# A hybrid decoder layer on eight cores: x0 first on the DMA engines, w_up casts moved out of the way of tile 3's residuals, and new engines for the last additions

## The chip, the cores and the metric

One Trainium2 chip, all 8 cores, one launch. Each core computes the same program on its own share of the tokens, with no traffic between cores. The metric is the device time in microseconds (us) of the slowest core. Some executions fall into a slow state, in which the cores of one die (cores 0 to 3 or 4 to 7) show a lower granted clock and run some per cent longer. Fast runs are compared with fast runs.

## The reference, cut to what matters

One layer: a token mixer (pooling and short convolution, merged by sigmoid gates), then a gated ConvFFN, each between two RMS norms.

```python
h = rmsnorm(x, g_pre_mix)
z = h @ w_in                                   # 1024 -> 4096 columns: 32 blocks of 128
... pooling mixer a, short convolution b ...
merged = sigmoid(ga) * a + sigmoid(gb) * b
x = x + rmsnorm(merged @ w_o, g_post_mix)      # needs x again: the residual
h = rmsnorm(x, g_pre_ffn)
upc = causal_dwconv(h @ w_up)                  # 44 blocks of 128 columns, in 22 pairs gate/value
y = (silu(gate) * val) @ w_down
x = x + rmsnorm(y, g_post_ffn)
```

All inputs are fp32. Weights become bf16 on their way into the core's memory, by casting DMAs that GpSimd issues.

## The kernel before

A core has 2080 tokens, in five tiles for the mixer (tile 0 of 512 tokens, tiles 1 to 4 of 392) and six for the FFN (344 each, without the first 16 tokens). A small scheduler orders the operations per engine; `after=[...]` holds one back until another is done. `L` is 4, the last mixer tile. Cuts are marked.

```python
def wload(buf, src, m, after=()):      # one casting DMA of a weight block, issued by GpSimd (L482)
    ...
def wup(n):                            # the next n of the 44 w_up blocks
    ...
    for k in range(i, hi):
        pool_dma(W_UP.ap(k), w_up[k], [], [W_UP.t(k)], 128 * BL * 4, mx=2048, after=[last_pe[0]])

# the start: x0 in five pieces through SP, w_in through GpSimd, 60 warm-up matmuls
PARTS0 = ((0, 2), (2, 2), (4, 2), (6, 1), (7, 1))
...                                    # xs0[q]: the load of piece q
wload(W_IN, w_in, 0)
warm(60)
for i in range(1, 16):
    wload(W_IN, w_in, i, after=[last_pe[0] if i < 3 else xs0[1]])
... w_pool, w_in 16 to 31, w_co, then tile 1's x in four plain loads, all after xs0[1] ...

def B(t):                              # merge: gates, sigmoids, products
    for m in range(8):
        ...
        merge(t, m, *g[m])
        if t == L:
            wup(1)

for i in range(16):                    # the input projection of the last tile
    F_block(L, i)
    wup(1)
    if i == 4:
        WO(L - 1)                      # tile 3's output projection
        epi(L - 1)                     # its norm and residual: loads x of tile 3 again through GpSimd
small_states()
B(L)
WO(L, split=True, hook=lambda: wup(1))
...
for t in range(NTB):                   # the FFN
    for j in range(FC):                # 22 pairs
        pair(t, j)                     # reads w_up blocks 2j and 2j+1
        if t == 0:
            wup(1)
        if 20 <= 22 * t + j < 28:
            epi_x(L, 22 * t + j - 20)
        if (t, j) in ((0, 9), (0, 11), (0, 14), (0, 16), (0, 19), (0, 21), (1, 1), (1, 3)):
            wdn()                      # one of 8 w_dn blocks, 704 KB each
        ...
# the last additions: chunks 0,1 by an accumulating DMA, 2,3 by GpSimd, 4 to 7 by VectorE in PSUM
steps = ((0, 2, None, "acc"), (2, 2, None, "pool"), (4, 2, 0, "dve"), (6, 2, 2, "dve"))
```

All matmuls have line L469, since one helper records them.

## Time and profile before

Median 821.01 us (820.97 to 821.67). The spans in the traces below are shorter than the times of the same runs (820.1 against 821.65 here). I cut each core's span at five landmarks and averaged each stretch over the eight cores:

| stretch | before, us |
|---|---|
| start to first gate after tile 0 (L700) | 68.7 |
| to the end of tile 3's output projection (L732) | 214.8 |
| to the first pair of the FFN (L817) | 56.2 (core 0: 57.7) |
| to the last normalisation, after the last matmul (L520) | 467.6 |
| to the end of the span | 11.2 |

This is the view by tile, core 7 of the kernel before, from 340 to 400 us. It gives the number of issues with their shortest, median and longest duration in ns, the first and the last issue, and the time to landing.

```profile
L482 POOL DMA_DIRECT2D big<-w_up x12: 713/747/750, 341.5 to 369.1; - x12
DMA to landing us min/median/max: 7.3/10.8/14.2
```

The last block goes out at 369.1 us and lands at 378.9. The pair that reads it, pair 21, begins at about 388 us on this core (I count the 16 matmuls of each pair from the first at 338.35 us): 9 us to spare, and 8 to 10 us over the cores. No core spends any time waiting for w_up.

### The profile page before, as it was taken

The numbers are of one execution on the slowest core, as the hardware profiler recorded it, in microseconds if no ns is written. First come the engines' busy times: TensorE is split into PE (matmuls) and PEld (weight loads), VectorE is DVE, ScalarE is ACT, GpSimd is POOL, SyncE is SP. The second block draws the span as 40 slices with busy tenths as digits, with TensorE's granted clock in tenths as the row PEclk, the third lists the DMA queues.
The fourth block names the chain that finished last, engine by engine and source line by source line (L and its number), as shares of the span: only waits on it lengthen the run. The fifth ranks groups of instructions, "written<-read, shape, count | busy, mean of one in ns | idle before, by whom it ended". The sixth has DMA issues, their size and how long they took to land.

```text
span 820.1 us, 16719 instructions; the slowest of 8 cores (817.4 to 820.1 us)
## 1 busy us (share of the span) xinstructions
PE 798.2 (97%) x5118; PEld 498.9 (61%) x5118; DVE 563.4 (69%) x1054; ACT 450.7 (55%) x903; POOL 259.9 (32%) x296
## 2 busy tenths in 40 slices
PE   7999999999999998999999999999999999999994
PEld 5454455555555554666666666666666666666662
DVE  3896547877977595588986486568566765785722
ACT  3533375676475544686754475456556555765532
POOL 6542002002101261499532252225222522242221
PEclk9999999999999999999999999999999999999998
DMA  9999706567117799999960132015101500040063
GB/s 182 201 160 156 152 20 136 148 164 157 41 36 158 109 171 208 169 159 171 183 113 1 35 46 53 1 36 70 36 2 36 70 2 1 6 66 2 1 133 77
DMA packets 63735, 75.18 MB, mean 92 GB/s; under 512 B 3072, under 2 KB 59264, under 8 KB 63632
## 3 DMA queue, kind: packets, MB, share of 16 engines
q0 software_dynamic: 41440, 44.97, 38.9%
q1 hardware_dynamic: 22208, 29.14, 12.8%
q8 instruction: 44, 0.72, 0.3%
q14 instruction: 43, 0.35, 0.2%
HBM read 81.53 MB, written 22.90 MB: 127 GB/s over the span
## 4 chain that ended last, share of the span: by engine, by line
PE 90%; DMA 4%; DVE 2%; issue 2%; POOL 1%; ACT 1%; DVEq 0%; ACTq 0%; POOLq 0%
PE ps L469 90%; DMA big<-xT 4%; POOL big L482 1%; DVE big L549 0%; DVE big L783 0%; DVE big L821 0%; ACT big L520 0%; DVE big L509 0%; DVEq L1078 0%; DVE big L578 0%; ACT L520 0%; DVE big L658 0%; DVE big L867 0%; ACT big L848 0%; ACT big L768 0%
## 5 line engine op out<-in xcount | busy, mean ns | idle before, releaser
L469 PE MATMUL ps<-big 128*128 128x346 bf16 (+5 forms) x5118 | 798.2, 319 | 10.6 <-POOL big L922 2.9
L469 PEld LDWEIGHTS ps<-big 128*128 128x128 bf16 x5118 | 498.9, 98 | 309.6 <-issue 15.8
L821 DVE SCALAR_TENSOR_TENSOR big<-ps,big 128x344 f32<-128x344 f32 (+1 forms) x528 | 281.1, 569 | 94.8 <-ACT big L817 74.9
L835 POOL TENSOR_TENSOR big<-big 128x344 bf16<-128x344 f32 x132 | 125.5, 952 | 258.5 <-DVE big L821 186.2
L817 ACT ACTIVATE big<-ps,big 128x344 f32<-128x344 f32 (+1 forms) x264 | 139.4, 541 | 67.5 <-PE ps L469 61.7
L834 ACT ACTIVATE big<-big 128x344 f32<-128x344 f32 x132 | 64.6, 489 | 47.9 <-DVE big L821 45.9
L700 ACT ACTIVATE big<-ps 128x392 f32<-128x392 f32 (+1 forms) x80 | 38.9, 512 | 51.8 <-PE ps L469 34.7
L480 POOL DMA_DIRECT2D big<-xT x16 | 15.8, 997 | 153.4 <-DVE big L713 147.0
L845 ACT ACTIVATE big<-ps,big 128x344 f32<-128x344 f32 x48 | 26.0, 546 | 58.8 <-PE ps L469 55.8
L482 POOL DMA_DIRECT2D big<-w_up x44 | 33.3, 758 | 64.6 <-PE ps L469 52.8
L713 DVE SCALAR_TENSOR_TENSOR big<-ps,big 128x392 f32<-128x392 f32 (+1 forms) x40 | 25.8, 645 | 33.7 <-PE ps L469 31.4
L509 DVE TENSOR_TENSOR big<-big 128x1568 bf16<-128x1568 bf16 (+3 forms) x28 | 24.5, 875 | 32.2 <-ACT big L732 26.0
L851 DVE TENSOR_TENSOR big<-big 128x688 bf16<-128x688 bf16 x17 | 8.8, 518 | 41.5 <-ACT big L848 41.5
L480 POOL DMA_DIRECT2D yT<-big x21 | 27.3, 1523 | 31.0 <-DVE big L867 17.3
L730 ACT ACTIVATE big<-ps,big 128x392 f32<-128x392 f32 (+1 forms) x40 | 24.5, 613 | 13.0 <-PE ps L469 12.9
L606 DVE TENSOR_TENSOR big<-big 128x406 f32<-128x406 f32 (+7 forms) x50 | 29.8, 598 | 1.5 <-ACT big L628 0.2
L482 POOL DMA_DIRECT2D big<-w_in x32 | 23.2, 743 | 20.6 <-DMA big<-w_in 10.9
L575 ACT ACTIVATE big<-big 128x392 f32<-128x392 f32 (+1 forms) x20 | 12.7, 638 | 30.6 <-DVE big L664 30.5
L768 ACT ACTIVATE big<-big 128x784 bf16<-128x784 f32 (+1 forms) x20 | 17.8, 891 | 18.5 <-DMA big<-xT 16.0
L578 DVE SCALAR_TENSOR_TENSOR big<-big 128x392 f32<-128x392 f32 (+1 forms) x40 | 25.5, 644 | 3.6 <-ACT big L575 3.0
L848 ACT ACTIVATE big<-ps 128x344 bf16<-128x344 f32 x48 | 21.6, 451 | 10.4 <-PE ps L469 10.2
L719 DVE TENSOR_TENSOR big<-big 128x392 bf16<-128x392 f32 (+1 forms) x40 | 24.9, 631 | 2.3
(62 smaller groups left out, 353.4 us busy)
## 6 DMA issues: line engine op xcount, KB each, us to landing
big<-w_up POOLq DMA_DIRECT2D x44, 256.0 KB, 10.0
big<-w_in POOLq DMA_DIRECT2D x32, 256.0 KB, 22.6
yT<-big POOLq DMA_DIRECT2D x21, 344.0 KB, 6.2
big<-xT POOLq DMA_DIRECT2D x16, 392.0 KB, 8.9
yT<-big SPq DMA_DIRECT2D x8, 784.0 KB, 8.5
big<-w_dn POOLq DMA_DIRECT2D x8, 704.0 KB, 14.1
big<-xT SPq DMA_DIRECT2D x6, 784.0 KB, 6.2
big<-h2T SPq DMA_DIRECT2D x6, 692.0 KB, 5.8
```

The costliest lines, as they stand in the source:

```text
L469: ins = e.matmul(o, lhsT=l, rhs=x, start=(start and i == 0), stop=(stop and i == last))
L480: return S.add("pool", lambda e: e.dma_start(out=out, in_=in_, accum_op=ALU.add, max_dma_last_dim=mx), r, w, dma=True, byts=byts, pri=pri, ...
L482: return S.add("pool", lambda e: e.dma_start(out=out, in_=in_, max_dma_last_dim=mx), r, w, dma=True, byts=byts, pri=pri, after=after)
L578: dve(lambda e, k=k: e.scalar_tensor_tensor(out=cv, in0=p[:, 2 + k + lo:2 + k + N], scalar=cc(C_WC + 4 * k + c), in1=cv, op0=ALU.mult, op1 ...
L606: dve(lambda e, nx=nx, cur=cur, s=s, a2=a2: e.tensor_tensor(out=nx[:, a2:W], in0=cur[:, a2:W], in1=cur[:, a2 - s:W - s], op=ALU.add), [ct] ...
L700: act(lambda e, b=b, g=g: e.activation(out=GT[t].ap[:, g, lo:N], in_=bank(b, N, lo), func=AF.Sigmoid), [("ps", b)], [GT[t].t(g, 1)], N, ps ...
L713: dve(lambda e: e.scalar_tensor_tensor(out=A_, in0=bank(bp, N, lo), scalar=cc(C_PS + m), in1=A_, op0=ALU.mult, op1=ALU.mult), [("ps", bp), ...
L817: act(lambda e, b=b, fj=fj, tt=tt: e.activation(out=tt[:, 0:n], in_=bank(b, n), func=AF.Copy, scale=cc(C_WF + fj)), [("ps", b), KCST], [to ...
L821: dve(lambda e, b=b, fj=fj, tt=tt, k=k: e.scalar_tensor_tensor(out=tt[:, 0:n], in0=ps[:, b * 512 + k:b * 512 + k + n], scalar=cc(C_WF + 44 ...
L834: act(lambda e: e.activation(out=g, in_=g, func=AF.Silu), [T.t(0, 1)], [T.t(0, 1)], NB, tab="silu")
L835: S.add("pool", lambda e: e.tensor_tensor(out=gb.ap[:, j, :], in0=g, in1=v, op=ALU.mult), [T.t()], [gb.t(j, 1)], dur=NB * 2.17 + 100)
L845: act(lambda e: e.activation(out=Y.ap[:, m, :], in_=bank(b, NB), func=AF.Copy, scale=cc(C_G4 + m)), [("ps", b), KCST], [Y.t(m, 1)], NB, ps ...
```

## The change

The intent: let x0's first half have the DMA engines to itself; keep w_up casts out of GpSimd's queue while tile 3's residuals are loaded through the same queue; spread the work of `epi_x` among the first pairs of FFN tile 1; and end without an accumulating DMA.

```diff
-            steps = ((0, 2, None, "acc"), (2, 2, None, "pool"), (4, 2, 0, "dve"), (6, 2, 2, "dve"))
+            steps = ((0, 2, None, "pool"), (2, 1, None, "pool"), (4, 2, 0, "dve"), (6, 2, 2, "dve"), (3, 1, 4, "dve"))
... (the "acc" branch removed)
-    wload(W_IN, w_in, 0)
     warm(60)
-    for i in range(1, 16):
-        wload(W_IN, w_in, i, after=[last_pe[0] if i < 3 else xs0[1]])
+    for i in range(16):
+        wload(W_IN, w_in, i, after=[xs0[1 if i else 0]])
@@ merge loop
-            if t == L:
-                wup(1)
+            if t == L and m > 0:
+                wup(2)
@@ last tile
     for i in range(16):
         F_block(L, i)
-        wup(1)
+        if i < 7:
+            wup(1)
@@ pairs
+    EPX = (20, 21, 22, 23, 25, 26, 28, 29)
-            if 20 <= 22 * t + j < 28:
-                epi_x(L, 22 * t + j - 20)
+            if 22 * t + j in EPX:
+                epi_x(L, EPX.index(22 * t + j))
... (the last load of X1 takes all 8 chunks instead of 6)
```

More of the change, by code (lines that the diff above doesn't have):

```diff
@@ L872, in epi_y @@
                 yk, xk = Y.ap[:, k:k + n, :], X1.ap[:, k:k + n, :]
-                if how == "acc":
-                    pool_dma(yT[:, k:k + n, lo:lo + NB], yk, [Y.t(k, n)] + [("y", a, 0) for a in tiles_a(lo, lo + NB)],
-                             [("yo", t, k)], 2 * 128 * n * NB * 4, acc=True)
-                    continue
                 if how == "pool":
@@ L1065, in build_nc @@
     lo = T0B + (NTB - 1) * NB
-    sp_dma(X1.ap[:, 2:8, :], yT[:, 2:8, lo:lo + NB], [("y", a, q) for a in tiles_a(lo, lo + NB) for q in range(2)],
-           [X1.t(2, 6)], 128 * 6 * NB * 4)
+    sp_dma(X1.ap, yT[:, :, lo:lo + NB], [("y", a, q) for a in tiles_a(lo, lo + NB) for q in range(2)],
+           [X1.t()], 128 * KC * NB * 4)
     for m in range(8):
```

## The prediction

> **What bounds the kernel now.** I read the list of cores first, since the slowest core sets the time:
>
> ```profile
> core 0: 820.1 us, clock 0.994
> core 3: 819.0 us, clock 0.996
> core 7: 819.0 us, clock 0.995
> ```
>
> The eight spans run from 817.4 to 820.1 us; the timed 821.0 is the slowest span plus 0.9. The page gives TensorE 798.2 busy of 820.1 us, so everything else is worth at most the other 21.9 us. The table of waits says where TensorE stands still (line, releaser, us in total, times, longest), and the chain in order of time (start, length, what) says how two of those waits came about:
>
> ```profile
> PE ps L469 <- POOL big L922: 2.9, 1, 2.9
> PE ps L469 <- DVE big L509: 2.3, 1, 2.3
> PE ps L469 <- ACT big L940: 1.8, 2, 1.1
> PE ps L469 <- DVE big L964: 1.1, 1, 1.1
> ...
> PE ps L469 <- DVE big L821: 0.9, 1, 0.9
> ```
>
> The chain:
>
> ```profile
> 14.39 12.74 DMA big<-xT
> ...
> 29.53 7.14 PE ps L469 x42
> ...
> 298.36 19.45 DMA big<-xT
> ...
> 318.84 0.99 DVE big L509
> ...
> 320.63 80.94 PE ps L469 x525
> ```
>
> L940 squares the pieces of tile 0, L964 scales tile 1: both wait for transfers. The L509 wait of 2.3 us ends at 320.63: the last residual transfer of tile 3 took 19.45 us. The same residuals of tile 2, with nothing beside them, took 7.7 us (median of the DMA view, 180 to 192 us). The slices of 2 us after that wait (window, its length, PE busy, weight loads, DVE, ACT, POOL, then the granted clock, DMA share, GB/s) show a second cost:
>
> ```profile
> 318.00:320.00 2.00, 0.34 (x3) 0.00 (x0) 1.05 (x2) 1.51 (x3) 0.34 (x1) 1.00 0.91 110
> 320.00:322.00 2.00, 1.36 (x8) 0.84 (x9) 1.90 (x4) 0.00 (x0) 0.00 (x0) 0.95 1.00 156
> 322.00:324.00 2.00, 2.00 (x7) 0.91 (x6) 0.71 (x2) 1.66 (x2) 0.00 (x0) 0.50 1.05 186
> 324.00:326.00 2.00, 2.00 (x10) 1.04 (x9) 1.08 (x3) 1.88 (x4) 0.72 (x1) 0.70 1.09 224
> 326.00:328.00 2.00, 2.00 (x14) 1.18 (x13) 2.00 (x5) 1.81 (x4) 0.00 (x0) 1.00 1.11 296
> ```
>
> The clock is 0.50 and 0.70 in two slices: [...]from the clocks, 0.1+1.0+0.6 = 1.7 us. I take 1.5. The other seven cores wait 0.8 to 1.8 us at this place and keep clock 1.00. Core 0 is the slowest because of this place.
>
> [...]the 512 KB quarters of x0 go through SP at 205 and 192 GB/s (4 to 6 and 6 to 8 us) while a w_in cast issued by GpSimd at 1.6 us is in flight, against 339 GB/s at 26 to 28 us. [...]casts and residuals share GpSimd's queue and the residuals stand behind w_up casts. The trace agrees: 7.7 us grew to 9.6, 11.4, 15.8 and 19.4 us. [...]Here 2.29 us of idling was followed by clock 0.50, and 1.8 us on core 4 was not.[...] The tail shows 2.13 us for 688 elements on GpSimd against 0.87 on VectorE, 2.4 times.
>
> **The change part by part.**
>
> Start. Before, w_in block 0 goes out at 1.6 us beside x0, blocks 1 and 2 after the sixty warm-up matmuls (9.3 us), the rest when x0's second quarter lands. After, block 0 waits for the first quarter (landed 4.9 us) and all others for the second. Core 0 sees the second quarter at 10.1 us; alone, at 340 GB/s, 1.18 MB (two quarters and the constants) from 2.2 us on take 3.5 us and[...] arrive at 6.6. The remaining 1.05 MB then share with casts: I expect the last of x0 near 11.5 instead of 13.3 us. Is TensorE then fed? Casts land one block per 1.67 us (block 1 at 16.1, block 7 at 26.1)[...]: block 1 is needed at 16.3 and lands 0.2 us before. So TensorE rides on the stream of casts, and x0 landing sooner helps only as far as the stream does too. The stream can win what the DMA wasted: from 2 to 14 us it moved 226 GB/s x 12 = 2.71 MB, that is 2.23 MB of x0 and constants (6.6 us at 340) and 0.48 MB of casts (3.1 us at 155), 9.7 us of work in 11.8 us of activity: 2.1 us of slack. TensorE's own floor is similar: warm-ups and sums as written let block 1's matmuls start at about 13.9, 2.4 us sooner. I count 1.9 us; tile 1 queues behind the same casts, so its 1.1 us wait stays, moved forward.
>
> Tile 3. w_up blocks 7 to 15 leave the F blocks of the last tile; 14 go out in the merge loop, two per step from the second step, and 15 instead of 12 in the first pairs. The residuals are issued at 293 to 298 us as before (they wait for VectorE's L760), but only two casts are sent in the 10 us before them. At tile 2's spacing (2 us apart) the fourth lands at about 305, squares and tree add 3.5 us: ready at 308.5. The order of instructions puts the sums some 37 matmuls (6 us) earlier, near 312, so there is no wait. Gain: core 0 2.3 + 1.5 = 3.8 us, the others 0.8 to 1.8. Seven cores also show 0.5 us behind the sigmoids (L700) just after, when ACT switches tables; core 0 may get that too.
>
> The pairs after it. GpSimd gets three more issues (3 x 0.75 us) where it is already 26.9 busy of 27 us (365 to 392). The order shows tile 4's sums 16 matmuls later and VectorE's eight L783 nearer together (4, then 7 L821, then 4; before 4, 11, 4), although they were to be spread. The 0.9 us wait on L821 stays or grows slightly: I count 0.2 us of loss.
>
> Tail. The accumulating DMA goes. VectorE multiplies the same 8 chunks and adds 5 instead of 4 (L882: 0.8 us per two, so +0.4); GpSimd adds 2+1 chunks, 2.13 + 1.07 us, from about 811.1 to 814.3, where it now ends at 814.43. SP issues five stores instead of three at 0.48 us each, in order: the last starts near 815.8 instead of 815.5, but is half as large and the first leaves a microsecond sooner. The same 1.41 MB goes out without the accumulate. Gain 0.2 us.
>
> **Sum.** Core 0: 820.1 - 1.9 - 3.8 + 0.3 (a sigmoid wait) + 0.2 - 0.2 = 814.7. Core 7: 819.0 - 1.9 - 1.1 + 0.2 - 0.2 = 816.0, core 3 by its 1.7: 815.4. The slowest is then another core, near 816; plus 0.9, rounded with a few tenths for the spread of starts: 817.0 us, 0.5% faster.
>
> **Rivals.** (a) The start is bound by DMA work, not order: the engines show shares of 0.82 to 1.18 from 4 us on, and casts beside x0's second half waste as before. Then the start gives 0 to 0.5 and the time is 818.5. (b) The moved casts hurt: 14 casts at 1.67 us fill the 24 us of the merge loop completely, beside 2 x 784 KB stores and the load of h2 (17 us to landing even before, landing at 330 where the pairs begin at 340.6), with 8 more in the output projection. A late h2, or GpSimd holding pair buffers, would cost 1 to 3 us: 819 to 820. For it speaks GpSimd's full stretch; against it the 10 us of spare on h2, and block 29 onward is first needed at pair 14, over 30 us after the first pair. (c) The waits in the start all go, clocks stay full and the tail gives 0.8: 814.
>
> **Range and chances.** The start may give 0 to 3, tile 3 on the slowest core 1 to 3.8, the rest -1.5 to +0.8. So 817.0 us, 8 in 10 between 814.3 and 819.8. Two per cent would be 804.6 or 837.4 us: faster needs 16 us, nearly all of TensorE's idle time with the tail, slower needs a new stall of 16 us where spare is 10 us. One chance in a hundred each.
>
> **What would show it.** Right: x0's second quarter landing before 7.5 us, F block 1 starting near 14.4 instead of 16.3; no L509 wait near 312, residuals landing in 8 to 9 us, clock 1.00 from 316 to 330 on every core; core 0 no longer slowest by a microsecond; the L821 wait near 0.9 still there. Wrong: waits on w_in after 14 us that eat the earlier start, a TensorE wait on h2 or a w_up block after the last projection, a wait on L821 above 2 us, or a last store landing more than 11.3 us after the last matmul.

The sum above came to 814.7 us for core 0 and 816.0 for core 7, and to 817.0 as the forecast. The 1.5 us of half clock was taken between the 1.7 us from the clocks and a lower figure from a count of matmuls. In the start, 2.2 and 3.5 us make 5.7, not 6.6: the rest was the allowance for landing. From the traces: a matmul of 392 columns took 166 ns at clock 1.00 (533 in 88.55 us up to the L509 wait, core 0 of the kernel before), eight of some 500 columns 1.7 us (68 in 14.65 us from 13.74 us); a cast of 256 KB in 1.67 us is some 155 GB/s; residuals and w_up casts moved on one queue (q0, 1.52 of 1.53 MB from 290 to 300 us); the switch of tables took 1.28 us (L700 at 324.77 us, core 4).

## The result, and the profile after

The changed kernel takes 826.77 us (median of four, 826.04 to 827.73), against 821.34 us for the kernel before in the same session. The ratio is 1.0062 with a 95% interval of 1.0042 to 1.0082. (Ratios are the mean time of one kernel's fast runs over that of the other's of the same rounds, so not quite the ratio of the medians.) It is slower, by less than 2%, where 0.5% faster was predicted. The range ended at 819.8.

The same stretches, mean of eight cores (differences taken before rounding):

| stretch | before | after | difference |
|---|---|---|---|
| start to first gate | 68.7 | 68.2 | -0.5 |
| to the end of tile 3's projection | 214.8 | 214.7 | -0.1 |
| to the first pair | 56.2 | 53.9 | -2.3 (core 0: -3.84) |
| to the last normalisation | 467.6 | 476.2 | **+8.7** |
| to the end | 11.2 | 10.2 | -1.0 |
| span | 818.5 | 823.2 | +4.7 |

Start, tile 3's stretch and tail gained 3.8 us together. The pairs lost more than twice as much. The list of cores of the changed kernel (the three that matter):

```profile
core 0: 823.9 us, clock 0.990
...
core 6: 819.8 us, clock 0.994
core 7: 824.5 us, clock 0.992
```

Clocks are lower than before (0.994 to 0.996), although no die is disturbed. TensorE's waits on core 7 (line, releaser, us in total, times, longest):

```profile
PE ps L469 <- DMA big<-w_up: 6.8, 1, 6.8
PE ps L469 <- ACT big L935: 1.9, 3, 0.9
PE ps L469 <- DMA big<-w_in: 1.6, 3, 0.9
...
PE ps L469 <- DVE big L509: 0.9, 1, 0.9
```

The first line is new: one wait of 6.8 us for a w_up block. (The remaining 0.9 us of L509 ends at 264.97 us. From there TensorE runs to the new wait without a stop.) The chain in order of time (start, length, what) around it:

```profile
371.95 21.22 DMA big<-w_up
393.17 0.35 issue
393.52 6.54 PE ps L469 x27
```

A block issued at 371.95 us landed 21.22 us later. GpSimd's transfers landed in the order of their issues in both traces, on every core (142 a core in the kernel before, 141 in the changed one). So what the block stood behind is in GpSimd's instructions in order of time (the w_up and w_dn issues from 362 to 377 us):

```profile
362.58 0.91 POOL L482 DMA_DIRECT2D big<-w_dn  x1
...
370.18 0.90 POOL L482 DMA_DIRECT2D big<-w_dn  x1
...
371.95 0.75 POOL L482 DMA_DIRECT2D big<-w_up  x1
...
375.39 0.74 POOL L482 DMA_DIRECT2D big<-w_up  x1
```

These last two w_up issues carry blocks 42 and 43, the blocks of pair 21. A w_dn block (704 KB in the core's memory, against 256 KB) goes out 1.8 us ahead of block 42; it is the second one ahead of these two blocks, where the kernel before has one. The view by tile, w_up and then w_dn, shows how far the queue had fallen behind:

```profile
L482 POOL DMA_DIRECT2D big<-w_up x15: 713/742/747, 340.1 to 375.4; - x15
...
DMA to landing us min/median/max: 13.3/17.4/21.2
...
L482 POOL DMA_DIRECT2D big<-w_dn x6: 898/919/928, 362.6 to 398.8; - x6
...
DMA to landing us min/median/max: 17.6/22.2/25.0
```

The median w_up block took 17.4 us to land, against 10.8 before, and the last ones 19 to 21. Finally the slices of 2 us around the wait (window, length, PE busy, weight loads, DVE, ACT, POOL, then granted clock, DMA share, GB/s):

```profile
386.00:388.00 2.00, 0.71 (x5) 0.26 (x3) 1.24 (x3) 1.81 (x5) 2.00 (x3) 1.00 1.11 130
...
392.00:394.00 2.00, 0.48 (x2) 0.29 (x3) 0.00 (x0) 0.00 (x0) 1.17 (x2) 0.50 1.15 271
394.00:396.00 2.00, 2.00 (x8) 1.05 (x7) 0.00 (x0) 0.00 (x0) 0.00 (x0) 0.50 1.19 169
396.00:398.00 2.00, 2.00 (x8) 1.05 (x7) 1.05 (x2) 0.55 (x1) 0.00 (x0) 0.50 1.14 137
398.00:400.00 2.00, 2.00 (x14) 1.28 (x12) 0.89 (x3) 1.61 (x4) 0.92 (x1) 0.88 1.18 152
```

After the wait TensorE ran at half clock: 8 matmuls a slice instead of 16. From its restart at 393.52 us that loses half of 0.48 + 2 + 2 + 0.48 us, 2.5 us. Wait and slow clock make 9.3 us on core 7, and its stretch of pairs grew by 9.2 us (467.07 to 476.31). (The L821 wait of 0.9 us went at the same time, so about 0.8 us of growth has other causes: 0.3 us is a wait near 787 us that grew from 0.69 to 0.99 us, the rest I did not look for.) All eight cores show this wait, 4.9 to 7.2 us.

Where w_up casts made way, the change did what it was to do. Core 0 of the changed kernel, two of the slices that the prediction shows for the kernel before:

```profile
320.00:322.00 2.00, 2.00 (x14) 1.18 (x13) 2.00 (x5) 0.43 (x1) 0.72 (x2) 1.00 0.90 147
322.00:324.00 2.00, 2.00 (x14) 1.18 (x13) 2.00 (x5) 0.99 (x2) 0.70 (x1) 1.00 1.07 177
```

TensorE is full at clock 1.00, with 14 matmuls in each slice where there were 8 and 7. The four residual transfers landed in 5.3 to 7.9 us instead of up to 19.45.

At the start, GpSimd's issues of core 7 (start, length), and TensorE after them with its idle time in brackets:

```profile
5.81 0.90 POOL L482 DMA_DIRECT2D big<-w_in  x1 [4.46 <-DMA big<-xT]
9.15 5.14 POOL L482 DMA_DIRECT2D big<-w_in  x7 [2.44 <-DMA big<-xT]
14.29 2.22 POOL L482 DMA_DIRECT2D big<-xT  x4
```

```profile
13.92 2.28 PE L469 MATMUL ps<-big 128*128 128x500 bf16 x10 [0.89 <-DMA big<-w_in]
...
22.18 7.08 PE L469 MATMUL ps<-big 128*128 128x512 bf16 x32 [0.39 <-DMA big<-w_in]
30.60 5.63 PE L469 MATMUL ps<-big 128*128 128x392 bf16 x33 [1.34 <-DVE big L676]
```

On this core x0's second quarter landed at 8.6 us and the last of x0 at 12.85. But the seven casts of w_in start at 9.15 us (9.35 in the kernel before) and tile 1's x goes out at 14.29 (14.54): the long queue of casts moved by 0.2 us. TensorE's first wait, for memsets that GpSimd used to do after issuing block 0, fell from 2.9 to 1.4 us; but its waits for pieces of x0 (L940 before, L935 after) grew from 1.1 to 1.9 us, and those for w_in blocks from 0.7 to 1.7 us.

### The profile page after: what moved, and what is told of

Read it like the earlier page. It is cut to its first block, busy times and chain, and to the rows that moved or that the text cites. A ratio compares the mean times of both kernels' runs of the same rounds, so it can differ in the third digit from the quotient of the medians.

```text
span 824.4 us, 16705 instructions; the slowest of 8 cores (819.8 to 824.5 us)
## 1 busy us (share of the span) xinstructions
PE 798.6 (97%) x5114; PEld 498.8 (61%) x5118; DVE 562.9 (68%) x1056; ACT 453.2 (55%) x903; POOL 259.0 (31%) x296
## 4 chain that ended last, share of the span: by engine, by line
PE 91%; DMA 5%; issue 1%; DVE 1%; POOL 1%; ACT 1%; DVEq 0%; SPq 0%; ACTq 0%; POOLq 0%
PE ps L469 91%; DMA big<-w_up 3%; DMA big<-xT 2%; POOL big L482 1%; DVE big L821 0%; ACT big L817 0%; DVEq L1075 0%; DVE ps L867 0%; ACT big L848 0%; POOL big L835 0%; SPq L476 0%; DVE big L676 0%; DVE big L867 0%; DVE big L878 0%; DVE big L578 0%
## 5 line engine op out<-in xcount | busy, mean ns | idle before, releaser
L821 DVE SCALAR_TENSOR_TENSOR big<-ps,big 128x344 f32<-128x344 f32 (+1 forms) x528 | 281.8, 569 | 104.8 <-ACT big L817 84.0
L817 ACT ACTIVATE big<-ps,big 128x344 f32<-128x344 f32 (+1 forms) x264 | 140.5, 542 | 80.9 <-PE ps L469 75.2
L700 ACT ACTIVATE big<-ps 128x392 f32<-128x392 f32 (+1 forms) x80 | 39.4, 514 | 56.5 <-PE ps L469 35.0
L509 DVE TENSOR_TENSOR big<-big 128x1568 bf16<-128x1568 bf16 (+3 forms) x28 | 23.7, 847 | 30.6 <-ACT big L732 28.6
L549 DVE SCALAR_TENSOR_TENSOR big<-big 128x392 bf16<-128x392 f32 (+1 forms) x40 | 24.2, 645 | 5.6 <-ACT big L526 5.6
L783 DVE SCALAR_TENSOR_TENSOR big<-big 128x392 bf16<-128x392 f32 (+1 forms) x40 | 24.8, 661 | 2.7 <-ACT big L523 2.7
## 6 DMA issues: line engine op xcount, KB each, us to landing
big<-w_up POOLq DMA_DIRECT2D x44, 256.0 KB, 15.7
```

What stands on the lines that cost most here:

```text
L700: act(lambda e, b=b, g=g: e.activation(out=GT[t].ap[:, g, lo:N], in_=bank(b, N, lo), func=AF.Sigmoid), [("ps", b)], [GT[t].t(g, 1)], N, ps ...
L817: act(lambda e, b=b, fj=fj, tt=tt: e.activation(out=tt[:, 0:n], in_=bank(b, n), func=AF.Copy, scale=cc(C_WF + fj)), [("ps", b), KCST], [to ...
L821: dve(lambda e, b=b, fj=fj, tt=tt, k=k: e.scalar_tensor_tensor(out=tt[:, 0:n], in0=ps[:, b * 512 + k:b * 512 + k + n], scalar=cc(C_WF + 44 ...
```

## The experiments

My theory after the traces: the casts that left the last tile's blocks became a backlog in GpSimd's DMA queue that lasted until the end of the first 22 pairs. There, w_dn loads stood in front of the last two w_up blocks. The rivals: the pairs lost to something else in the change (the start, or the spread `epi_x`); GpSimd issued the last casts too late (373.1 to 375.4 us over the cores, against 368.1 to 370.4 before); the w_dn loads alone are at fault.

The first four kernels ran on a chip whose die 0 stayed disturbed in every run (about 850 us). For them I compare cores 4 to 7 alone: the mean over runs of the slowest of these four, and of their mean. (Their clock, 0.98 to 0.99, is below the 0.995 of a quiet chip, in the kernel before as in the others.) The kernel before has 823.84 and 822.32 there (11 runs).

**1. w_up as before, the rest changed.**

```diff
-            if t == L and m > 0:
-                wup(2)
+            if t == L:
+                wup(1)
-        if i < 7:
-            wup(1)
+        wup(1)
```

> The changed kernel with the w_up casts issued as before (one per F block of the last tile, one per merge step). Theory (the 9 casts held back are what costs): the 6.8 us wait on w_up at the end of the first round of pairs and the half clock after it (about 1.9 us) go; the wait on L509 near 318 us (0.8 to 2.3 us by core) comes back; start (0.6 us) and tail (1.0 us) stay as gains. Time 819.7 us, 1.6 under the kernel before. Rival (the loss comes from the new start or from the spread of the eight L783): time stays within 1 us of the changed kernel's 826.8.

Measured: 822.56 and 821.12, so 1.2 us below the kernel before. No wait on w_up; the L509 wait is back (1.5, 0.4, 2.7 and 2.5 us on cores 4 to 7). Start, tail and `epi_x` do no harm: the loss comes from the w_up casts.

**2. w_dn later, the rest as changed.**

```diff
-            if (t, j) in ((0, 9), (0, 11), (0, 14), (0, 16), (0, 19), (0, 21), (1, 1), (1, 3)):
+            if (t, j) in ((0, 15), (0, 16), (0, 17), (0, 19), (0, 20), (0, 21), (1, 1), (1, 3)):
```

> The changed kernel with the eight w_dn loads moved behind the last w_up cast in GpSimd's queue (first at pair 15 instead of pair 9). Theory (the last w_up casts land late because the DMA is backed up and two to three w_dn loads of about 4.6 us each stand in front of them): the last two w_up blocks land 9 us or more sooner, near 384 us, before they are needed at 386.7; the wait and the half clock go. Time 818.0 us. Rival (GpSimd issues the last casts too late, w_dn does not matter; casts alone already took 13 to 15 us to land): 1 to 3 us of wait remain, time 820 to 823. Second rival: w_dn then lands too late for its first use in the next round and the wait turns up there, time 820 or more.

(The 4.6 us was an estimate. In the trace of the changed kernel a w_dn block landed 4.3 to 6.6 us, in the median 5.0 us, after the w_up block ahead of it.)

Measured: 820.70 and 819.68, so 2.6 to 3.1 us below the kernel before. No wait on w_up, none on L509 near 312 us, and no wait on w_dn took their place.

**3. The w_up part alone, on the kernel before.** The two hunks of the first experiment, the other way round.

```diff
-            if t == L:
-                wup(1)
+            if t == L and m > 0:
+                wup(2)
-        wup(1)
+        if i < 7:
+            wup(1)
```

> The kernel before with only the new places of the w_up casts. Theory: no L509 wait near 318 us and no half clock there (first pair 2.6 us sooner on average, 3.8 on core 0), but the wait on w_up of 6 to 7 us near 388 us and half clock after it. Time 828.3 us, 7 over the kernel before. Rival (the loss needs the other parts of the change too): within 2 us of the kernel before.

Measured: 829.42 and 827.49, so 5.2 to 5.6 us above the kernel before, with waits on w_up of 1.1, 7.1, 6.1 and 3.5 us on cores 4 to 7. Core 5:

```profile
PE ps L469 <- DMA big<-w_up: 7.1, 1, 7.1
```

The moved casts by themselves make as large a loss as the whole change.

**4. Hold the casts back from F block 10 on, instead of 7.**

```diff
-        if i < 7:
+        if i < 10:
             wup(1)
```

> The changed kernel with the casts held from F block 10 on instead of 7, so three more casts (5 us of DMA) go out before tile 3's residuals, and every later cast one place sooner. Theory (backlog): the last casts land at least 5 us sooner and with one w_dn less in front, so no or under 1 us of wait on w_up; the residuals land up to 3 us later, still before the sums need them, no L509 wait above 0.5 us. Time 818.0 us. Rival (the last casts are late for another reason than the amount of DMA work behind 308 us): wait still 4 us or more, time 823 or more.

Measured: 821.10 and 820.08, so 2.2 to 2.7 us below the kernel before. No wait on w_up on cores 4 to 7, and none on L509 near 312 us: six blocks held back instead of nine already clear the residuals. This edit changes two things at once: the backlog is three casts shorter, and one w_dn block goes out ahead of the last two w_up blocks instead of two.

The next four ran on a quiet chip, where the kernel before took 822.04 us (median of 11; mean of its fast runs 822.00). From here on the times given first are medians of all runs, a slow one or two among them except in experiment 7; ratios and fast means leave those out.

**5. The start alone, on the kernel before.**

```diff
-    wload(W_IN, w_in, 0)
     warm(60)
-    for i in range(1, 16):
-        wload(W_IN, w_in, i, after=[last_pe[0] if i < 3 else xs0[1]])
+    for i in range(16):
+        wload(W_IN, w_in, i, after=[xs0[1 if i else 0]])
```

> The kernel before with the change's start alone (w_in block 0 behind x0's first quarter, all other blocks behind its second). Theory, that the start is bound by the work of the DMA engines: the first gate after tile 0 comes about 0.6 us sooner than in the kernel before, TensorE waits 1 to 2 us for w_in block 0, the L509 wait near 320 us stays, no wait on w_up; time 0.3 to 0.8 us below the kernel before. Rival, the prediction's term: the first gate 1.5 to 2 us sooner and the time 1.5 to 2 us lower.

Measured: 821.93 us, ratio 1.0003 (0.9987 to 1.0020). The first gate comes at 68.57 us in the mean of the cores, 0.1 us sooner than in the trace of the kernel before. TensorE's waits on w_in are 1.3 to 2.2 us. The start gives nothing that these runs can resolve. The interval leaves room for my 0.3 to 0.8 us, but not for the 1.5 to 2 us of the rival.

**6. The last additions alone, on the kernel before.** The "acc" branch goes too, and the last load of X1 takes all chunks.

```diff
-            steps = ((0, 2, None, "acc"), (2, 2, None, "pool"), (4, 2, 0, "dve"), (6, 2, 2, "dve"))
+            steps = ((0, 2, None, "pool"), (2, 1, None, "pool"), (4, 2, 0, "dve"), (6, 2, 2, "dve"), (3, 1, 4, "dve"))
```

> The kernel before with the change's last additions alone (no accumulating transfer; GpSimd adds two chunks and one, VectorE five). Theory, from the traces: last L520 to the end of the span shrinks by about 1.0 us, from about 11.2 to 10.2, and the time with it. Rival, the prediction's term: 0.2 us.

Measured: 821.58 us, ratio 0.9995 (0.9982 to 1.0008). In the trace the last normalisation is followed by 10.1 us, against 11.2. In the timed runs the mean of the cores' spans falls by 0.45 us only (818.23 to 817.78), which the interval doesn't tell from nothing. The slowest cores are still picked by L509 (2.5 us on core 2, 3.0 on core 6).

**7. The second experiment's kernel again.** Its edit is that of experiment 2, unchanged.

> The changed kernel with the eight w_dn loads moved so that six stand behind pairs 15 to 21 instead of pairs 9 to 21; its first run met a disturbed die. Theory, that the last w_up casts were late because the backlog and the w_dn loads stood in front of them: no wait on w_up, the time 2 to 4 us below the kernel before (on a quiet chip 817 to 819), so 7 us or more below the changed kernel. Rival, that the changed kernel lost its time by anything else: 825 us or more with or without the wait.

Measured: 817.55 us (816.78 to 817.66), ratio 0.9943 (0.9931 to 0.9955): 4.5 us below the kernel before, with no wait on w_up on any core. It beats both kernels. The slowest core of its trace took 815.3 us, and all clocks are 0.995 or above. Its w_up view on core 7:

```profile
L482 POOL DMA_DIRECT2D big<-w_up x14: 716/742/750, 340.7 to 373.8; - x14
...
DMA to landing us min/median/max: 9.7/16.3/20.9
```

The backlog is still there (median 16.3 us), and the last issue is as late as in the changed kernel. But with w_dn behind it, block 43 lands 9.7 us after its issue, at 383.5, ahead of its pair. So GpSimd's late issue by itself is not the cause. Nor are the w_dn loads by themselves: in the kernel before one stands ahead of the last two w_up blocks too, and no core waits. It takes the backlog and the w_dn loads together.

**8. The same with w_in block 0 issued at once.** To the kernel of experiment 7:

```diff
-        wload(W_IN, w_in, i, after=[xs0[1 if i else 0]])
+        wload(W_IN, w_in, i, after=[xs0[1]] if i else [])
```

> As the run before it in this list, with w_in block 0 issued at once and not behind x0's first quarter. Theory, that the start is bound by the sum of the DMA work: within 0.4 us of that run, with x0's second quarter 1 us or more later. Rival, that block 0's late arrival alone eats the gain of the start: 1.0 to 1.5 us faster.

Measured: 817.97 us; the means of the fast runs are 817.58 and 817.33. First gate 68.4 us against 68.3. Whether block 0 goes first or x0 does makes no difference.

The last three ran on a third chip, whose die 1 had a clock of 0.987 in all kernels. There the kernel before took 825.81 us (fast mean 825.64), its die 0 a mean of 818.20.

**9. Both cures: experiments 2 and 4 together.** To the kernel of experiment 7:

```diff
-        if i < 7:
+        if i < 10:
```

> The changed kernel with both cures: w_up casts held back only from F block 10 on, and the w_dn loads moved behind pairs 15 to 21. Theory, that either cure alone takes the whole wait away: nothing more to win, so within 0.5 us of each cure alone (about 4.5 us below the kernel before on a quiet chip), no wait on w_up, no L509 wait near 312 us. Rival, that some lateness remains with one cure: 1 us or more below the better cure.

Measured: 822.76 us, ratio 0.9964 (0.9951 to 0.9977). On die 0, with a full clock, the mean is 814.74, 3.5 us below the kernel before. Experiment 7 on its chip has 3.4 by the same four cores. Nothing more was to be won than by w_dn alone.

**10. All of w_in behind x0's first quarter.** To the kernel of experiment 7:

```diff
-        wload(W_IN, w_in, i, after=[xs0[1 if i else 0]])
+        wload(W_IN, w_in, i, after=[xs0[0]])
```

> The changed kernel with w_dn late, and all of w_in behind x0's first quarter instead of its second, so that GpSimd starts its stream of casts 3 to 4 us sooner. Theory, that the start is bound by the DMA work: x0 lands later and TensorE waits for it, the first gate moves by less than 0.5 us. Rival, that the start is bound by the moment at which the stream of casts begins: the first gate 1.5 us or more sooner and the time 1.5 us or more lower than with the stream behind the second quarter.

Measured: 822.90 us, ratio 0.9962 (0.9949 to 0.9975); die 0 at 814.34, 3.9 below the kernel before. GpSimd issues w_in from block 1 on some 2 us sooner (block 1 at 6.5 to 8.0 us over the cores, where experiment 7 has 8.0 to 9.9), in one stream with block 0, as its issues on core 7 show:

```profile
7.02 6.09 POOL L482 DMA_DIRECT2D big<-w_in  x8 [5.67 <-DMA big<-xT]
13.08 2.23 POOL L482 DMA_DIRECT2D big<-xT  x4
```

Yet block 1 lands at 15.7 to 16.8 us, no sooner than in experiment 7 (15.7 to 16.9), and the first gate comes at 68.6 us (68.5 on die 0) against 68.3. Issuing sooner doesn't help. This fits a start that is bound by the work of the DMA engines, whichever way it is ordered; no run changes the amount of that work, so the bound itself is likely and not shown.

**11. The fourth experiment's kernel again.** Its edit is that of experiment 4, unchanged.

> The changed kernel with the w_up casts held back only from F block 10 on; its first run met a disturbed die. Theory, that a smaller backlog alone suffices although the w_dn loads still stand in front of the last casts: 4 to 5 us below the kernel before, no wait on w_up. Rival, that w_dn is the cause by itself: a wait on w_up of several us remains and the time is 823 us or more.

Measured: 823.67 us, ratio 0.9973 (0.9960 to 0.9986), so 2.3 us below the kernel before by the means of the fast runs (823.33 against 825.64): less than expected. Seven cores show no wait on w_up. In the traced run core 1 stands still for 2.8 us in pair 21, where the changed kernel did, after 8 of the pair's 16 matmuls: there block 43 is first read. Its TensorE in order of time, and then its last w_up block, issued at 366.0 us:

```profile
389.04 81.22 PE L469 MATMUL ps<-big 128*128 128x346 bf16 x543 [2.81 <-ACT big L817]
```

```profile
DMA to landing us min/median/max: 22.7/22.7/22.7
```

The block landed at 388.7 us, and TensorE went on 0.3 us later. (The same 0.35 us lie between landing and restart in the chain of the changed kernel.) The profile puts the wait down to ScalarE, whose L817 ended 0.1 us before the restart. Both fit the time, so I take the late block as likely and not as shown.

When the last w_up block landed (fast traces of cores with a full clock). Pair 21 begins at 384 to 387 us in these traces, in the kernel before at 387 to 389; its second half, over 1 us later, reads this block:

| kernel | last issue, us | landing, us |
|---|---|---|
| before | 368.1 to 370.4 | 377.0 to 379.0 |
| changed | 373.1 to 375.4 | 391.7 to 395.2 |
| w_dn late (7) | 372.6 to 375.1 | 380.4 to 383.6 |
| hold from 10 (11, die 0) | 365.8 to 366.0 | 381.7 to 388.7 |
| both (9, die 0) | 364.2 to 365.9 | 376.1 to 380.6 |

Holding from block 10 with w_dn in front leaves 1 to 4 us, and on one core none: it is the riskier cure. That core's wait is not all that it loses, though. On die 0 it takes 0.9 us more than both cures together (mean of the cores 815.59 against 814.74), and in its trace cores 0, 2 and 3, which don't have the wait, stand 0.3 us longer at L821 and 0.3 us longer near 777 us.

## Why the prediction was wrong, point by point

**The step that failed** is the answer to rival (b). It let the moved casts be harmless because "block 29 onward is first needed at pair 14, over 30 us after the first pair". That is true of block 29, and beside the point. The question was when the last block is needed and what stands ahead of it. I counted GpSimd's issues and the casts inside the merge loop ("14 casts at 1.67 us fill the 24 us of the merge loop completely") and stopped at its end. I did not carry the backlog on through the pairs, where 15 more w_up casts and the w_dn loads share one queue. The runs put in its place: +8.7 us in the pairs (mean of the cores), on each core a wait of 4.9 to 7.2 us for the blocks of pair 21, and half clock after it. The part alone costs it (experiment 3), taking it back removes it (1), and so does taking w_dn out of its way (2, 7). Rival (b) named the right danger, looked for it at h2 and at GpSimd's buffers, and sized it at 1 to 3 us. (Among the signs of being wrong the prediction did list a wait on a w_up block, and that is the sign that came.)

The trace that was available held the warning. In the kernel before the last w_up block had 9 us to spare, and its profile page gives the DMA engines a busy share of 90% or more in every slice from 287 to 410 us. The change moved nine casts, about 15 us of transfers at the 1.67 us per cast that the prediction itself used, to a place where the engines were already full. They also left a hole: on core 0 of the changed kernel nothing but the four residuals was issued from 286 to 300 us, and the engines' share from 288 to 296 us was 0.4, where it had been 1.0 to 1.2.

**Start, -1.9: the size was wrong.** Traces show -0.5 (changed kernel) and -0.1 (experiment 5), and the times show nothing. The term took x0's second quarter to land at 6.6 us at 340 GB/s. On core 7 of the changed kernel it landed at 8.6, and the casts behind it could then start hardly sooner than the old ones had. With no cast in flight before 5.8 us, the engines moved 276 GB/s there (2 to 5.8 us), not 340. The prediction misread its two rates: 205 and 192 GB/s are all transfers of those slices together, not x0's, and the 339 at 26 to 28 us is tile 1's x. F block 1, which was to start near 14.4 us, started at 16.8 on core 0, since block 1 of w_in landed at 16.7. Rival (a), 0 to 0.5 us, was right; experiments 8 and 10 show that the order of block 0 or of the whole stream doesn't matter.

**Tile 3, -3.8 on core 0 and -0.8 to -1.8 on others: right.** Core 0 gained 3.84 us in this stretch, the others 1.4 to 2.4, some 0.5 us more than predicted, since their wait behind the sigmoids (L700) went too; wait and half clock went, and residuals landed in 5.3 to 7.9 us, where 8 to 9 was predicted.

**L821, +0.2: wrong sign.** The wait of 0.9 us was to stay or grow. Core 7 of the changed kernel shows none, experiment 7 shows 0.4 to 0.5, experiments 9 and 11 show 0.8 and 1.1 on their die 0. With the same spread of `epi_x` it thus lies between nothing and 1.1 us, so it depends on what comes before it; no run isolates it.

**Tail, -0.2: too small.** The traces show -1.0. GpSimd was to finish its additions when it had before. In the kernel before it finished 5.6 us after the last normalisation began (814.43 less 808.85), as it had first to issue the accumulating DMA (1.22 us from 811.54). In the changed kernel on core 7 the additions took 2.50 us together, not 2.13 + 1.07, and ended after 4.7 us. How much of that microsecond reaches the time stays open: experiment 6 shows 0.4 us, within its uncertainty.

**The sum.** With the late blocks cured, the change makes 817.55 us, close to the predicted 817.0. That is partly luck: 1.4 us or more too much for the start against 0.8 too little for the tail and 0.6 for L821. And the step from the slowest span to the time, taken as 0.9 us, was 2.1 in the mean of that kernel's five runs.

## What to carry to other kernels

When transfers are moved later to make room, follow the queue on to the last transfer's deadline, with everything that is issued ahead of it, and not only to the end of the stretch that was cleared. A look at the landing time of the last block before the change (here 9 us of spare, against 15 us of transfers moved) says how much may be moved. And if one load has a distant deadline (w_dn) and stands in front of one with a near deadline, swapping the two is the better cure here: it cost nothing here and turned a loss of 5.4 us into a gain of 4.5.

## What the traces show of waits, order and casts

- Idle time and the clock after it. After 2.29 us of waiting on core 0 of the kernel before the granted clock was 0.50 and 0.70 in the slices from 322 to 326 us; after 2.81 us on core 1 of experiment 11 it was 0.69 and 0.50 from 388 to 392 us; after the 6.8 us on core 7 of the changed kernel 0.50 from 392 to 398 us. After 1.84 us on core 4 of the kernel before it stayed at 1.00 from 320 to 328 us. These runs do not show what decides.
- Order in GpSimd's queue. w_up blocks issued 1.8 and 5.2 us after a w_dn block landed only at 393.2 and 394.8 us, after that block's 390.2, and the last one 9.7 us after issue once w_dn stood behind it (experiment 7). On core 7 of the changed kernel a w_up cast of 256 KB issued from 340 us on took 13 to 21 us to land.
- Rates. At the start one block cast to bf16 landed per 1.67 us, some 155 GB/s written, against up to 339 GB/s for the plain loads of tile 1's x (core 0 of the kernel before, 26 to 28 us). A block is 512 KB in fp32 where it is read, so the reading side moves some 310 GB/s (an estimate from the 1.67 us). By that estimate most of the difference is that a cast writes half of what it reads.
